# Weight blocks side by side instead of in pairs, moving tiles 96 bytes higher, and v normalised in eight pieces

## The chip, the core and the metric

The kernel runs on one core of a Trainium2 chip. The metric is the device time of one execution in microseconds: 2833.92 us is the median of three runs of the kernel before (2832.6 to 2835.17).

Five engines work side by side: TensorE (matmuls, PE in the profile; its weight loads are listed apart as PEld), VectorE (DVE), ScalarE (ACT), GpSimd (POOL) and SyncE (SP), which issues most of the DMAs. Data lies in a memory of 128 partitions (SBUF); matmuls write to another one (PSUM).

## What is computed

One step of a two-layer streaming encoder in float32, on 256 frames of a new stream and 32 frames of a running one, 288 columns in all, of width 2048. Layer 0 mixes frames with a gated MLP (gMLP), layer 1 with a multi-scale retention; each is followed by a SwiGLU network of hidden width 5632, and each of the four sublayers by a residual and a LayerNorm.

```python
def gmlp_mix(x, w_in, ln_g, ln_b, w_s, b_s, w_out):
    z = jax.nn.gelu(x @ w_in, approximate=False)
    u, v = jnp.split(z, 2, axis=-1)
    v = layer_norm(v, ln_g, ln_b)
    ...
    mixed = jnp.einsum('gts,bnsgc->bntgc', w, vg) + bias
    s = u * mixed.reshape(bsz, t, GMLP_HALF)
    return s @ w_out, v

def swiglu(x, w_in, w_out):
    gate, up = jnp.split(x @ w_in, 2, axis=-1)
    return (jax.nn.silu(gate) * up) @ w_out

def trunk(...):
    for i in range(DEPTH):
        if i % N_MIXERS == 0:
            h, v = gmlp_mix(...)
        else:
            h, s = retention_mix(...)
        x = layer_norm(ALPHA * x + h, ln_mix_g[i], ln_mix_b[i])
        x = layer_norm(ALPHA * x + swiglu(x, w_ffn_in[i], w_ffn_out[i]), ln_ffn_g[i], ln_ffn_b[i])
```

## The kernel before

**Weights.** All matrices are cut into blocks of 128 x 128, and the host packs them, in the order in which the kernel uses them, into chunks of eight (`CB`). `Core.prep` loads a chunk of 512 KB with a DMA on SP's queue into a tile `raw` (three buffers), and `split` makes two tiles of it in a shorter float32 format that TensorE takes in one pass (`F32R`): `whi` is the rounded chunk, made by ScalarE, and `wlo` what is left of it, made by VectorE. Both have four buffers, and a chunk is prepared three chunks ahead of its use.

**Matmuls.** `step` multiplies one weight block with one 128-row slice of the activations, which exist as a pair of tiles as well (`xh`, `xl`): three matmuls, hi by hi (L106), hi by lo (L107) and lo by hi (L108), summed into the same PSUM bank. Each has a block of weights of its own to load, so there is a load for every matmul. `Core.tiles` and `Core.group` run the steps over all slices of an output tile of 128 rows. After each output tile a clock of the program, `tick`, runs what was put off with `after(n, ...)`, n output tiles ahead.

**Where the bytes lie.** A block of weights is not contiguous in its chunk: blocks 2i and 2i+1 share 256 columns, the one taking the even columns and the other the odd ones (L89); the host packs them so. The activations that stream through TensorE, called moving tiles, have rows of 320 floats (`ROW`) of which the first four are left free (`LEAD`). A step of 288 columns reads such a row turned: `turned` (L168) takes four floats, leaves out eight, and so on, three times over the row, and writes the results to PSUM in the same order. Steps of 290 columns carry two columns more, for the gain and bias of a LayerNorm that is corrected after the matmul; they read the row straight. These are the first twelve output tiles after each of three LayerNorms. Tiles that nobody reads, such as `shift` with 64 floats, move all tiles that are allocated behind them: `xh`, `xl`, `y`, and the tiles of the gMLP, the retention and the ffn. The pool of the weights is allocated earlier.

**The gMLP's v.** The 16 output tiles of v come first, then those of u, all within layer 0's first matrix. v is transposed to rows through DRAM, its statistics are taken, and `v_norm` normalises it in quarters of 512 columns, for 32 and twice 128 rows: a scaling on ScalarE, a product with the gain and a sum with the bias on VectorE, and for the 32 rows of the running stream a split. Gain and bias come by a DMA on SP's queue into `gb`, two buffers. The first quarter is normalised at once, the others two, four and six output tiles later; four output tiles behind each quarter, `sample_mix` uses the running stream's part.

**What sets the order.** TensorE runs its instructions in the order of the code. On the other engines a scheduler puts the instructions in order when the program is built.

Of the kernel before, what the change touches and what calls it, by code (L numbers as in the profile page):

```python
# [10 lines left out]
F32 = mybir.dt.float32  # L11
# [8 lines left out]
P = 128  # L20
# [18 lines left out]
CB = 8  # L39
# [7 lines left out]
class Core:  # L47
# [33 lines left out]
    def blk(self, w, k, m):  # L81
        i = len(self.order)
        self.order.append((w, k, m))
        c, j = divmod(i, CB)
        if j == 0:
            self.prep(c + 3)
            self.ready.pop(c - 1, None)
        hi, lo = self.ready[c]
        return tuple(t[:, j // 2 * 2 * P + j % 2:(j // 2 + 1) * 2 * P:2] for t in (hi, lo))  # L89

    def state(self, h):

# [80 lines left out]
def rsqrt(nc, out, v, t):  # L173

    nc.vector.tensor_scalar(out.bitcast(I32), v.bitcast(I32), -0.5, float(0x5F3759DF), ALU.mult, ALU.add)
    for _ in range(3):
        newton(nc, out, out, v, t)
# [242 lines left out]
def moving(pool, n, name, tag=None):  # L420

    t = pool.tile([P, n, ROW], F32R, name=name, **({"tag": tag} if tag else {}))
    return t[:, :, LEAD:]


def split(nc, hi, lo, f):
    nc.scalar.copy(hi, f)  # L427
    nc.vector.tensor_tensor(lo, f, hi.bitcast(F32), ALU.subtract)  # L428
# [12 lines left out]
def gmlp(core, cst, x, y, lnp, ins, v_out, load):  # L441
# [3 lines left out]
    with ExitStack() as es:  # L445
        pool = es.enter_context(tc.tile_pool(name="gm", bufs=1, reuse_waits="tile"))
# [46 lines left out]
        def v_rows(q):  # L493
            for t in range(3):
                n = rows[t]
                nc.vector.bn_stats(st[:n, t, q, :], vt[t][:n, q * 512:(q + 1) * 512])
            if q == 3:
                v_stats()

        def v_stats():  # L500
            for t in range(3):
                n = rows[t]
                nc.vector.bn_aggr(nrm[:n, t, 0:2], st[:n, t, :, :].rearrange("p a b -> p (a b)"))
            mean, var, u, r, w, b = (nrm[:, :, i] for i in (0, 1, 2, 3, 4, 5))
            nc.vector.tensor_scalar(u, var, LN_EPS, None, ALU.add)
            rsqrt(nc, r, u, w)
            nc.vector.scalar_tensor_tensor(b, mean, -1.0, r, ALU.mult, ALU.mult)
            v_norm(0)
            for q in range(1, 4):
                core.after(2 * q, lambda q=q: v_norm(q))  # L510

        def v_norm(q):
            cs = slice(q * 512, (q + 1) * 512)
            gb = pool.tile([P, 2, 512], F32, tag="gb", name=f"gb{q}", bufs=2)
            nc.sync.dma_start(gb, ins["a_gb"][:, :, cs])
            for t in (2, 0, 1):
                n = rows[t]
                v = vt[t][:n, cs]
                nc.scalar.activation(v, v, AF.Identity, bias=nrm[:n, t, 5:6], scale=nrm[:n, t, 3:4])
                nc.vector.tensor_tensor(v, v, gb[:n, 0, :], ALU.mult)  # L520
                nc.vector.tensor_tensor(v, v, gb[:n, 1, :], ALU.add)
                if t == 2:
                    split(nc, v3[:NS, cs], v3[NS:2 * NS, cs], v)
                    nc.scalar.copy(v3[2 * NS:, cs], v)
            core.after(4, lambda: sample_mix(q))
            if q == 3:
                nc.gpsimd.dma_start(v_out, vs[:NS, :])

        def sample_mix(q):

            ps = core.bank(f"smix{q}")
            for g in (2 * q, 2 * q + 1):
                w = w3[:, g].rearrange("p a n -> p (a n)")
                nc.tensor.matmul(ps[:, (g % 2) * 256:(g % 2 + 1) * 256], w, v3[:, g * 256:(g + 1) * 256], start=True, stop=True)
            view = ps.rearrange("p (m a s) -> p m a s", a=4, s=32)
            for a in range(4):
                r = slice(32 * a, 32 * a + 32)
                nc.vector.transpose(ms[r, 4 * q:4 * q + 4, :], view[r, :, a, :])
# [30 lines left out]
def ffn(core, cst, x, y, lnp, layer, prev, out=None):  # L569
    tc, nc = core.tc, core.nc  # L570
    xh, xl = x
    xs = lambda k: (xh[:, k, :NT], xl[:, k, :NT])
    ln = PostNorm(core, cst, x, y, lnp, 2 * layer + 1, out)
    with tc.tile_pool(name=f"ffn{layer}", bufs=1, reuse_waits="tile") as pool:
        hh = moving(pool, HH, f"hh{layer}")
        hl = moving(pool, HH, f"hl{layer}")
        for half in range(2):
            sg = {}

            def evac(m, ps):  # L580
                if m < HT:
                    t = pool.tile([P, NT], F32, tag="sg", name=f"sg{layer}_{m}", bufs=4)
                    nc.scalar.activation(t, ps[:, :NT], AF.Silu)
                    sg[m] = t
                else:
                    j = m - HT
                    i = j - half * HH
                    f = pool.tile([P, NT], F32, tag="hf", name=f"hf{layer}_{j}", bufs=3)
                    nc.vector.tensor_tensor(f, ps[:, :NT], sg.pop(j), ALU.mult)
                    split(nc, hh[:, i, :NT], hl[:, i, :NT], f)  # L590

            ms = []
            for j in range(half * HH, (half + 1) * HH):
                ms += [j, HT + j]
            if half == 0:
                prev.start(f"f_in{layer}", ms, evac)
                ms = ms[4 * RAW:]
            core.tiles(f"f_in{layer}", 0, list(range(KT)), ms, xs, evac, grouped=False)
            core.tiles(f"f_out{layer}", half * HH, list(range(HH)), list(range(KT)),
                       lambda k: (hh[:, k, :NT], hl[:, k, :NT]),  # L600
                       ln.last if half else ln.part)
    return ln
# [297 lines left out]
@with_exitstack  # L900
def hybrid_step(ctx, tc, ins, outs):
    nc = tc.nc
    ctx.enter_context(tc.manual_schedule(engines={PE}))
    core = Core(ctx, tc, ins["wpack"])
    cp = ctx.enter_context(tc.tile_pool(name="cp", bufs=1))
    lnp = ctx.enter_context(tc.tile_pool(name="lnp", bufs=1))
    cp.tile([P, 64], F32, name="shift")
    lnp.tile([P, 32], F32, name="shift_lnp")
    xh = moving(cp, KT, "xh")
    xl = moving(cp, KT, "xl")  # L910
    y = cp.tile([P, KT, NT], F32, name="y")
    cst = {}
    cp.tile([P, 32], F32, name="shift_one")
    cst["one2048"] = cp.tile([P, P], F32, name="one2048")
    nc.gpsimd.memset(cst["one2048"], 1.0 / D)
    cst["ln"] = cp.tile([P, 4, 2, KT], F32, name="lnv")
    cst["one_r"] = cp.tile([P, P], F32R, name="one_r")
    nc.scalar.copy(cst["one_r"], cst["one2048"])
    warm = core.bank("warm")
    for _ in range(11):  # L920
        nc.tensor.matmul(warm[:, :P], cst["one2048"], cst["one2048"], start=True, stop=True)

    def load(k):
        if k < KT:
            if k % 2 == 0:
                nc.sync.dma_start(y[:, k:k + 2, :], ins["xT"][:, k:k + 2, :])
            split(nc, xh[:, k, :NT], xl[:, k, :NT], y[:, k, :])

    with tc.manual_schedule(engines={mybir.EngineType.DVE, mybir.EngineType.Activation}):
        core.prep(0, lambda: load(0))  # L930
        for k in range(1, 4):
            load(k)
            core.prep(k)
    x = (xh, xl)
    ln = gmlp(core, cst, x, y, lnp, ins, outs["v"], lambda s: load(s + 4))
    ln = ffn(core, cst, x, y, lnp, 0, ln)
    ln = retention(core, cst, x, y, lnp, ln, ins, outs["st_p"], outs["st_s"])
    ffn(core, cst, x, y, lnp, 1, ln, outs["yT"])
    core.flush()
    assert len(core.order) == NBLK + NSTATE  # L940
    return core.order
# [85 lines left out]
```

## Time and profile before

| what | value |
|---|---|
| median of three runs | 2833.92 us (2832.6 to 2835.17) |
| profiled execution, first to last instruction | 2831.8 us |
| what lies around it, by the median | 2.1 us |
| TensorE busy | 2818.8 us, 21,574 matmuls |
| VectorE busy | 1696.5 us |
| ScalarE busy | 1241.5 us |
| moved by DMA | 515.49 MB, 182 GB/s on average |

The time of the profiled execution itself isn't given beside its span; the median less the span stands in for what lies around it. In a row of the groups, the number behind `x` counts the instructions, and behind the bar stand the time in which at least one of them ran, the mean duration of one in ns, and the idle time ahead of them. Names are those of the program: `af_in` is an output of a step in an ffn's first matrix, `aa_in` of the gMLP's, `ab_in` of the retention's. A matmul of float32 proper counts twice, since TensorE runs it in two passes. In a row of stretches, the number behind an engine's busy time counts the instructions that touch the stretch.

### The profile page before, as it was taken

To read this page: it belongs to the slowest core of one execution; us is meant where nothing else is said; L and a number is where in the kernel's file an instruction comes from. 1 tells how busy PE (TensorE), PEld (TensorE's weight loads), DVE (VectorE), ACT (ScalarE), POOL (GpSimd) and SP (SyncE) were. 2 spreads that over 40 slices of the span, in tenths; PEclk is the share of its full clock that TensorE was granted. 3 is DMA by queue.
4 is the path that set the end of the run, shared out by engine and by line. 5 is a ranking of instruction groups with operands and counts; after the bars stand their busy time and mean duration, and the time that the engine had idled before them with its cause. 6 is when DMAs were issued, how large, how long until landed. Compare 5 with 4: busy or idle time off the path is not lost.

```text
span 2831.8 us, 51419 instructions
## 1 busy us (share of the span) xinstructions
PE 2818.8 (100%) x21574; PEld 2804.0 (99%) x21574; DVE 1696.5 (60%) x2432; ACT 1241.5 (44%) x1642; POOL 141.4 (5%) x241
## 2 busy tenths in 40 slices
PE   9999999999999999999999999999999999999998
PEld 9999999999999999999999999999999999999998
DVE  5678864444444456777765666767854444444455
ACT  5544553333333344554443444444553333333343
POOL 1100000000000000012200111200000000000001
PEclk9999999999999999999999999999999999999999
DMA  8655555555555555567765666755555555555553
GB/s 281 208 177 164 166 167 172 171 171 170 170 168 171 174 174 173 174 207 230 226 195 169 195 214 214 223 190 170 164 171 170 170 170 171 171 172 172 171 170 125
DMA packets 146584, 515.49 MB, mean 182 GB/s; under 512 B 18016, under 2 KB 20336, under 8 KB 146320
## 3 DMA queue, kind: packets, MB, share of 16 engines
q1 hardware_dynamic: 131984, 473.47, 50.9%
q0 software_dynamic: 14224, 38.59, 4.5%
q8 instruction: 168, 2.75, 0.4%
q14 instruction: 64, 0.52, 0.1%
q10 hardware_dynamic: 144, 0.15, 0.0%
HBM read 486.98 MB, written 25.17 MB: 181 GB/s over the span
## 4 chain that ended last, share of the span: by engine, by line
PE 98%; DVE 1%; DMA 1%; ACT 0%; issue 0%; POOL 0%; SPq 0%; DVEq 0%; POOLq 0%; ACTq 0%
PE af_in L108 13%; PE af_in L107 13%; PE af_in L106 13%; PE ab_in L106 7%; PE ab_in L108 7%; PE ab_in L107 7%; PE af_out L107 6%; PE af_out L108 6%; PE af_out L106 6%; PE ab_out L108 2%; PE ab_out L106 2%; PE ab_out L107 2%; PE aa_in L108 2%; PE aa_in L107 2%; PE aa_in L106 2%; PE aa_out L108 1%
## 5 line engine op out<-in xcount | busy, mean ns | idle before, releaser
L428 DVE TENSOR_TENSOR wlo<-raw,whi 128x1024 fp32r<-128x1024 f32 (+1 forms) x892 | 1085.5, 1219 | 903.2 <-ACT whi L427 898.9
L427 ACT CAST whi<-raw 128x1024 fp32r<-128x1024 f32 (+1 forms) x892 | 933.0, 1048 | 1434.0 <-PE af_in L107 343.0
L107 PE MATMUL af_in<-xl,whi 128*128 128x288 f32 (+1 forms) x2816 | 825.1, 293 | 0.0
L108 PE MATMUL af_in<-xh,wlo 128*128 128x288 f32 (+1 forms) x2816 | 823.3, 292 | 0.0
L106 PE MATMUL af_in<-xh,whi 128*128 128x288 f32 (+1 forms) x2816 | 820.8, 291 | 0.0
L108 PEld LDWEIGHTS af_in<-xh,wlo 128*128 128x128 f32 x2816 | 550.5, 196 | 0.0
L107 PEld LDWEIGHTS af_in<-xl,whi 128*128 128x128 f32 x2816 | 545.8, 194 | 0.0
L106 PEld LDWEIGHTS af_in<-xh,whi 128*128 128x128 f32 x2816 | 544.1, 193 | 0.0
L108 PE MATMUL ab_in<-xh,wlo 128*128 128x288 f32 (+1 forms) x1536 | 449.6, 293 | 0.0
L106 PE MATMUL ab_in<-xh,whi 128*128 128x288 f32 (+1 forms) x1536 | 449.3, 293 | 0.0
L107 PE MATMUL ab_in<-xl,whi 128*128 128x288 f32 (+1 forms) x1536 | 447.7, 291 | 0.0
L107 PE MATMUL af_out<-hl,whi 128*128 128x288 f32 x1408 | 411.0, 292 | 0.0
L108 PE MATMUL af_out<-hh,wlo 128*128 128x288 f32 x1408 | 409.9, 291 | 0.0
L106 PE MATMUL af_out<-hh,whi 128*128 128x288 f32 x1408 | 409.8, 291 | 0.0
L106 PEld LDWEIGHTS ab_in<-xh,whi 128*128 128x128 f32 x1536 | 299.7, 195 | 1.1
L108 PEld LDWEIGHTS ab_in<-xh,wlo 128*128 128x128 f32 x1536 | 297.8, 194 | 0.0
L107 PEld LDWEIGHTS ab_in<-xl,whi 128*128 128x128 f32 x1536 | 296.8, 193 | 0.9
L108 PEld LDWEIGHTS af_out<-hh,wlo 128*128 128x128 f32 x1408 | 273.9, 195 | 0.0
L107 PEld LDWEIGHTS af_out<-hl,whi 128*128 128x128 f32 x1408 | 273.4, 194 | 0.0
L106 PEld LDWEIGHTS af_out<-hh,whi 128*128 128x128 f32 x1408 | 271.8, 193 | 0.0
L108 PE MATMUL aa_in<-xh,wlo 128*128 128x288 f32 x512 | 149.4, 292 | 1.1 <-DVE wlo L428 1.1
L107 PE MATMUL aa_in<-xl,whi 128*128 128x288 f32 x512 | 149.5, 292 | 0.1
(249 smaller groups left out, 2942.6 us busy)
## 6 DMA issues: line engine op xcount, KB each, us to landing
raw<-in_wpack_dram SPq DMA_DIRECT2D x887, 512.0 KB, 3.4
v_room<-tv POOLq DMA_DIRECT2D x32, 144.0 KB, 4.7
of<-o_room POOLq DMA_DIRECT2D x32, 144.0 KB, 4.4
vw<-v_room POOLq DMA_DIRECT2D x8, 512.0 KB, 5.6
out_st_s_dram<-sso POOLq DMA_DIRECT2D x16, 256.0 KB, 2.7
o_room<-to POOLq DMA_DIRECT2D x8, 512.0 KB, 3.9
out_st_p_dram<-so POOLq DMA_DIRECT2D x16, 256.0 KB, 5.5
y<-in_xT_dram SPq DMA_DIRECT2D x8, 288.0 KB, 5.0
```

What stands on the lines that cost most here:

```text
L106: mm(ps, hi, xh, start=first, stop=False)
L107: mm(ps, hi, xl, start=False, stop=False)
L108: mm(ps, lo, xh, start=False, stop=last)
L427: nc.scalar.copy(hi, f)
L428: nc.vector.tensor_tensor(lo, f, hi.bitcast(F32), ALU.subtract)
```

## The change

Three things are changed. The blocks of a chunk lie side by side, 128 contiguous columns each, in the kernel and in the host's packing (the blocks of the retention's state lay so before, and still do). `shift` has 88 floats instead of 64, which moves all tiles behind it by 96 bytes. And v is normalised in eight pieces of 256 columns, one after each of the next eight output tiles, with four buffers of half the size for gain and bias; `sample_mix` follows two output tiles after each second piece, and so at the same output tiles as before.

```diff
@@ blk
-        return tuple(t[:, j // 2 * 2 * P + j % 2:(j // 2 + 1) * 2 * P:2] for t in (hi, lo))
+        return tuple(t[:, j * P:(j + 1) * P] for t in (hi, lo))
@@ v_stats
-            v_norm(0)
-            for q in range(1, 4):
-                core.after(2 * q, lambda q=q: v_norm(q))
+            for i in range(8):
+                core.after(1 + i, lambda i=i: v_norm(i))
 
-        def v_norm(q):
-            cs = slice(q * 512, (q + 1) * 512)
-            gb = pool.tile([P, 2, 512], F32, tag="gb", name=f"gb{q}", bufs=2)
+        def v_norm(i):
+            cs = slice(i * 256, (i + 1) * 256)
+            gb = pool.tile([P, 2, 256], F32, tag="gb", name=f"gb{i}", bufs=4)
             nc.sync.dma_start(gb, ins["a_gb"][:, :, cs])
...
-            core.after(4, lambda: sample_mix(q))
-            if q == 3:
+            if i % 2:
+                core.after(2, lambda: sample_mix(i // 2))
+            if i == 7:
                 nc.gpsimd.dma_start(v_out, vs[:NS, :])
@@ hybrid_step
-    cp.tile([P, 64], F32, name="shift")
+    cp.tile([P, 88], F32, name="shift")
@@ kernel
-            pairs = wpack[c].reshape(P, CB // 2, P, 2)
-            pairs[:, j // 2, :, j % 2] = mats[w][k * P:(k + 1) * P, m * P:(m + 1) * P]
+            wpack[c, :, j * P:(j + 1) * P] = mats[w][k * P:(k + 1) * P, m * P:(m + 1) * P]
```

The order on TensorE and GpSimd is the same before and after. On VectorE, this stands before where v is normalised; `raw`, `whi` and `wlo` ending in 1524 to 1526 are chunk 42, `gb_1339` and `gb_1479` the first two quarters' gain and bias:

```order
L521 TENSOR_TENSOR y<-y,gb_1479 32x512
L520 TENSOR_TENSOR g_vp<-g_vp,gb_1479 128x512 x2
L428 TENSOR_TENSOR g_v_149<-y,g_v_149 32x512
L521 TENSOR_TENSOR g_vp<-g_vp,gb_1479 128x512 x2
L428 TENSOR_TENSOR wlo_1526<-raw_1524,whi_1525 128x1024
L428 TENSOR_TENSOR wlo_1559<-raw_1557,whi_1558 128x1024
L428 TENSOR_TENSOR wlo_1589<-raw_1587,whi_1588 128x1024
L538 STREAM_TRANSPOSE g_ms<-smix_1619 32x128 x4
```

Three chunks' splits follow each other behind two quarters. After, at the same place (`gb_1479` and `gb_1556` are now the second and third of eight, 1571 to 1573 is chunk 43):

```order
L520 TENSOR_TENSOR y<-y,gb_1479 32x256
L519 TENSOR_TENSOR g_vp<-g_vp,gb_1479 128x256 x2
L520 TENSOR_TENSOR g_vp<-g_vp,gb_1479 128x256 x2
L428 TENSOR_TENSOR g_v_149<-y,g_v_149 32x256
L428 TENSOR_TENSOR wlo_1526<-raw_1524,whi_1525 128x1024
L519 TENSOR_TENSOR y<-y,gb_1556 32x256
L519 TENSOR_TENSOR g_vp<-g_vp,gb_1556 128x256
L520 TENSOR_TENSOR y<-y,gb_1556 32x256
L520 TENSOR_TENSOR g_vp<-g_vp,gb_1556 128x256
L519 TENSOR_TENSOR g_vp<-g_vp,gb_1556 128x256
L428 TENSOR_TENSOR g_v_149<-y,g_v_149 32x256
L520 TENSOR_TENSOR g_vp<-g_vp,gb_1556 128x256
```

The split of chunk 42 still stands behind two pieces, which are half as wide; then comes the third piece, ahead of the split of chunk 43.

On SP's queue, before, the last two quarters' gain and bias stand together behind the loads of chunks 43 and 44:

```order
L73 DMA raw_1557<-in_wpack_dram 128x1024
L73 DMA raw_1587<-in_wpack_dram 128x1024
L515 DMA gb_1626<-in_a_gb_dram 128x2x512
L515 DMA gb_1776<-in_a_gb_dram 128x2x512
L73 DMA raw_1641<-in_wpack_dram 128x1024
L73 DMA raw_1671<-in_wpack_dram 128x1024
```

After, the last four of the eight are spread over five loads of chunks:

```order
L73 DMA raw_1601<-in_wpack_dram 128x1024
L514 DMA gb_1717<-in_a_gb_dram 128x2x256
L514 DMA gb_1804<-in_a_gb_dram 128x2x256
L73 DMA raw_1655<-in_wpack_dram 128x1024
L514 DMA gb_1888<-in_a_gb_dram 128x2x256
L73 DMA raw_1685<-in_wpack_dram 128x1024
L73 DMA raw_1732<-in_wpack_dram 128x1024
L514 DMA gb_1974<-in_a_gb_dram 128x2x256
L73 DMA raw_1762<-in_wpack_dram 128x1024
```

Each of these waits until a piece of v has freed its buffer; the loads of chunks 45, 46 and 48 now stand behind such a wait, where before the load of chunk 45 alone stood behind both.

## The prediction

> **What bounds the kernel now.** I read the page's first part and its chain of waits, then the groups of instructions by form, then stretches of single stages, and last the few places where a matmul of the main stream stands next to another kind.
>
> ```profile
> span 2831.8 us, 51419 instructions
> PE 2818.8 (100%) x21574; PEld 2804.0 (99%) x21574; DVE 1696.5 (60%) x2432; ACT 1241.5 (44%) x1642; POOL 141.4 (5%) x241
> PEclk9999999999999999999999999999999999999999
> PE 98%; DVE 1%; DMA 1%; ACT 0%; issue 0%; POOL 0%; SPq 0%; DVEq 0%; POOLq 0%; ACTq 0%
> ```
>
> TensorE is the path: 98% of the chain, at its full granted clock. So the time is the number of matmuls times their spacing, plus a head, a tail and a few waits. A matmul's recorded duration holds its pipeline too, so the spacing is taken from stretches of one stage.
>
> ```profile
> L107 PE MATMUL af_in<-xl,whi 128*128 128x288 f32 x2432 | 710.6, 292 | 0.0
> L108 PE MATMUL af_in<-xh,wlo 128*128 128x288 f32 x2432 | 708.8, 291 | 0.0
> L106 PE MATMUL af_in<-xh,whi 128*128 128x288 f32 x2432 | 706.4, 290 | 0.0
> ...
> L108 PE MATMUL ab_in<-xh,wlo 128*128 128x288 f32 x1344 | 392.6, 292 | 0.0
> ...
> L108 PE MATMUL af_in<-xh,wlo 128*128 128x290 f32 x384 | 114.5, 298 | 0.0
> ...
> L108 PE MATMUL ab_in<-xh,wlo 128*128 128x290 f32 x192 | 57.0, 297 | 0.0
> ...
> L294 PE MATMUL m<-s,one_r 128*128 128x288 f32 x16 | 2.8, 294 | 0.0
> ...
> L267 PE MATMUL cen<-cen,one_r 128*128 128x288 f32 x4 | 1.2, 295 | 0.0
> ```
>
> ```profile
> core 0: us, PE busy (x) PEld busy (x) DVE busy (x) ACT busy (x) POOL busy (x), PEclk, DMA share, GB/s
> 315.00:385.00 70.00, 70.00 (x522) 70.00 (x521) 56.68 (x97) 43.45 (x68) 0.58 (x1) 1.00 0.49 161
> 600.00:720.00 120.00, 120.00 (x933) 120.00 (x932) 59.91 (x70) 41.08 (x39) 0.00 (x0) 1.00 0.51 169
> ...
> 126.00:158.00 32.00, 30.88 (x239) 30.44 (x238) 30.36 (x49) 24.70 (x35) 0.51 (x1) 1.00 0.53 181
> ```
>
> The three lines of `step` (L106 to L108) run 7,040 times each, 21,120 matmuls in all (the code's NBLK: 512 + 256 + 1,536 + 512 + 4,224 blocks). Two forms occur. The 288-column form reads its moving tile turned (16 bytes, then a jump of 48); the 290-column form, at the start of the two ffn layers and of the retention, reads it straight, 3 x (384 + 192) = 1,728 times by the two groups above. That leaves 19,392 turned ones. From 600 to 720 us some 931 turned matmuls start (933 touch the stretch, two of them across its edges): 120 us / 931 = 128.9 ns each. From 315 to 385 us it is 70 us / 520 = 134.6 ns for a straight one. The difference, 5.7 ns, is about that of the durations, 298 against a mean of 291.3 over the groups of the turned form. So a duration in ns can serve as a yardstick for spacing where only a few rows exist: one ns longer is one ns later, and one ns on all step matmuls is 21.1 us, 0.75% of the time. The stretch of 600 to 720 us has VectorE busy half the time, that of 315 to 385 us four fifths, and both come out as steady as the group means; what the other engines do is not what sets the spacing.
>
> **The change part by part.** No matmul is added or removed, and TensorE's order stays as it is. What changes is which bytes each one reads.
>
> *Weight blocks side by side.* While a matmul streams, the weights of the next are loaded. Now these 128 columns lie 8 bytes apart over 1,024 bytes; then they lie 4 bytes apart over 512. No step matmul of this trace does that, so its price has to come from the neighbours. Other matmuls of the kernel have weights stored contiguously (the score, value and state products of the retention, the LayerNorm sums), and the last step matmul ahead of such a block is exactly the case wanted: turned moving data, and a contiguous load of 128 columns beneath it. These are three of the sixteen ahead of the output and state products, and one ahead of a load of 64 columns:
>
> ```profile
> L108 PE MATMUL ab_in<-xh,wlo 128*128 128x288 f32 x1 | 0.3, 294 | 0.0
> ...
> L820 PE MATMUL ob<-vv,ph 128*128 128x512 f32 x1 | 0.4, 388 | 0.0
> L108 PE MATMUL ab_in<-xh,wlo 128*128 128x288 f32 x1 | 0.3, 295 | 0.0
> ...
> L870 PE MATMUL sp<-vv,kh 128*128 128x512 f32 x1 | 0.4, 388 | 0.0
> L108 PE MATMUL ab_in<-xh,wlo 128*128 128x288 f32 x1 | 0.3, 295 | 0.0
> ...
> L107 PE MATMUL ab_in<-xl,whi 128*128 128x288 f32 x1 | 0.3, 291 | 0.0
> L108 PE MATMUL ab_in<-xh,wlo 128*128 128x288 f32 x1 | 0.3, 290 | 0.0
> ```
>
> They took 294, 295 and 295 ns (in the groups of single moments at 1251.3, 1859.5 and 1867.8 us), where the group of the same line has 292 and all turned ones 291.3; above the 64-column load (the last pair of rows, at 1243.6 us) it took 290. So the load is felt by the matmul above it, and a contiguous one more than a paired one. These rows give +2 to +3.7 ns.
>
> The straight form says the opposite. The LayerNorm sums have straight moving data of 288 columns and contiguous weights, and took 294 to 295 ns; the straight step matmuls have pairs, and took 297 to 298 with two columns more, which at 128.9 / 288 = 0.45 ns a column is 296.8 for 288. Side by side is cheaper there by some 2.3 ns. The loads themselves speak that way too:
>
> ```profile
> L106 PEld LDWEIGHTS af_in<-xh,whi 128*128 128x128 f32 x2816 | 544.1, 193 | 0.0
> L870 PEld LDWEIGHTS sp<-vv,kh 128*128 128x128 f32 x64 | 11.6, 188 | 2.1
> L820 PEld LDWEIGHTS ob<-vv,ph 128*128 128x128 f32 x48 | 8.6, 188 | 1.4
> ```
>
> A contiguous load takes 188 ns, a paired one 193 and more. But a load is begun a matmul ahead, and what counts is the matmul. So the price lies between -2.3 and +3.7 ns. I take +2.6 for the turned form (294.2 less the mean of 291.3 and the 292 of the same line), because those rows share the moving pattern with 19,392 of the 21,120, and -2.3 for the 1,728 straight ones: 19,392 x 2.6 ns = +50.4 us and 1,728 x -2.3 ns = -4.0 us.
>
> Here a rule of the Trainium skill speaks for no change at all: its page "TensorE: Matmul & The Clock Gate" (section "Step-by-step: what each phase is for") says that TensorE reads moving data and weights through two independent ports, so that loading the next weights takes nothing from the running matmul. By it this part costs 0 instead of the +46 us above. The rows of 290 and 294 to 295 ns do not agree with it.
>
> *Moving tiles 96 bytes higher.* `shift` grows from 256 to 352 bytes, and with it every later tile, among them all that the step matmuls stream and none of the weights, whose pool comes first. In the trace of before all streamed tiles of the step stand alike against the weights, since rows and tiles are multiples of 128 bytes long, so no row shows another distance. Its bounds are those of the whole pattern: nothing, down to the 2.3 ns that the straight rows would allow, or up to the loss of what turning wins, 296.8 - 291.3 = 5.5 ns. I take 0, nearest to the rows that I priced the load from, and keep 5.5 as the upper end.
>
> *v normalised in eight pieces.* The page's step of four pieces sits at 126 to 158 us, where the stretch above has TensorE busy for 30.88 of 32 us, and VectorE for 30.36.
>
> ```profile
> PE aa_in L108 <- DVE wlo L428: 1.1, 2, 1.0
> L428 DVE TENSOR_TENSOR wlo<-raw,whi 128x256 fp32r<-128x256 f32 x4 | 1.5, 420 | 3.8 <-ACT whi L427 3.8
> L521 DVE TENSOR_TENSOR g_vp<-g_vp,gb 128x512 f32<-128x512 f32 x8 | 5.4, 684 | 0.1
> 134.83 1.30 DVE L521 TENSOR_TENSOR g_vp<-g_vp,gb 128x512 f32<-128x512 f32 x2
> 136.04 2.35 DVE L428 TENSOR_TENSOR wlo<-raw,whi 128x1024 fp32r<-128x1024 f32 x2
> ```
>
> TensorE waits 1.1 us here for `wlo`, which VectorE makes only after two pieces of v in a row. Eight pieces make 56 instructions on VectorE instead of 28: 56 x 420 - 28 x 684 ns = +4.4 us in a stretch where VectorE has 1.6 us to spare, and about as many more on ScalarE, which has 7 us. Cover: the weights are prepared three chunks ahead, each 24 x 128.9 ns = 3.1 us long, and in the order of after the split of chunk 42 still stands behind two pieces, now of half the width. On SP's queue the loads of g and b become eight of half the size, and the later four each wait for a buffer that a piece of v has read, with the raw weights queued behind them; before, two did. If the wait only moves, nothing changes; if all the extra work is uncovered, +4.4 us; if the wait goes, -1.1. I take -1.
>
> **The sum.** +50.4 - 4.0 + 0 - 1 = +45.4 us. On the profiled execution's span of 2831.8 us that is 2877.2; the median of the three runs, 2833.92, stands 2.1 us above that span, so 2879 us, slower by 1.6%.
>
> **The rivals.**
>
> *The shorter load wins (faster).* If what the straight rows and the load rows show holds for the turned form as well, every step matmul gets 2.3 ns shorter: 21,120 x 2.3 = 48.6 us, so 2833.9 - 48.6 - 1 = 2784 us. For it: 188 against 193 ns, and 294.5 against 296.8. Against it: the rows of 294 and 295 ns above turned data. It decides from the point where the mean duration of the turned form falls below 291.0 (0.27 ns x 21,120 = 5.7 us).
>
> *Nothing happens (same).* The load is hidden whatever its layout, and only v moves: 2833 us. For it: the spacing of 128.9 ns is steady over the stages, so one could take it for a property of the streaming alone. Against it: the 290 of the 64-column load. This is what the rule of the two ports in the Trainium skill would give, and the page "SBUF — State Buffer" (section "Specifications (TRN2)", the row on cachelines) has both layouts read each line of 16 bytes at least twice, and so at full rate.
>
> *Turning loses its effect (much slower).* Turned data is 5.5 ns faster than straight under paired weights. That may rest on both streams stepping through the memory in a fixed relation, which the change breaks twice, by the other step of the weights and by the 96 bytes. Then a turned matmul costs what a straight one does: 19,392 x 5.5 = 106.7 us, 2833.9 + 106.7 - 4 - 1 = 2936 us. For it: the only known contrast of patterns in the trace is that large. Against it: the 294 and 295 ns, which keep half of the gain.
>
> **How the numbers follow.** My forecast has 0.66, the faster rival 0.14, no change 0.05, the loss of turning 0.12, and 0.03 is left for more than that. Within the forecast, between +1 and +4 ns a matmul, the time lies from 2850 to 2915 us. The range of 2830 to 2945 leaves out the faster rival and the last 0.03. A difference under 0.2% (5.7 us) can't be told from no change with this kernel. Slower is forecast, loss of turning and the rest, 0.81; same 0.05; faster 0.14.
>
> **What the profile after would show.** If the first part is right, the groups of L106 to L108 with 128x288 read 293 to 295 ns instead of 290 to 292, evenly over all stages; a stretch such as 600 to 720 us has some 914 matmuls instead of 933; the straight groups of 290 columns read about 295; the loads of L106 to L108 drop from 193 to about 188 ns; the wait of aa_in for `wlo` at 136 us is gone or half as long. The granted clock stays full, VectorE and ScalarE have the same work and lower shares. Durations below 291 mean the faster rival, of 296 or more the lost turning. If the three lines differ by more than now, the 96 bytes act on the streamed tile, and not the layout of the weights. What would make this wrong: the rows that I lean on are transitions between two kinds of matmul, not a steady stream, and a steady stream may settle into another rhythm.

## The result

The kernel after takes 2787.49 us (median of four runs, 2787.04 to 2790.12) against 2834.26 us of the kernel before: a ratio of 0.9834 with a 95% interval of 0.982 to 0.9848, so 1.7% faster. The forecast was 2879 us, slower. The time is within 4 us of the rival called "the shorter load wins" (2784 us), though the runs below show that its mechanism is not the one at work.

The profile after: the page's first part, its clock row and its chain of waits.

```profile
span 2787.7 us, 51475 instructions
PE 2775.6 (100%) x21574; PEld 2760.2 (99%) x21574; DVE 1698.1 (61%) x2460; ACT 1245.7 (45%) x1662; POOL 141.8 (5%) x241
PEclk9999999999999999999999999999999999999999
PE 98%; DVE 1%; DMA 0%; issue 0%; POOL 0%; ACT 0%; DVEq 0%; POOLq 0%
```

TensorE is the path as before, with as many matmuls, at its full granted clock, with 43 us less busy time. So the matmuls follow each other more closely. The groups by form of the kernel after, with one group of weight loads at the end:

```profile
L106 PE MATMUL af_in<-xh,whi 128*128 128x288 f32 x2432 | 701.1, 288 | 0.0
L107 PE MATMUL af_in<-xl,whi 128*128 128x288 f32 x2432 | 701.1, 288 | 0.0
L108 PE MATMUL af_in<-xh,wlo 128*128 128x288 f32 x2432 | 701.1, 288 | 0.0
...
L108 PE MATMUL af_in<-xh,wlo 128*128 128x290 f32 x384 | 113.5, 296 | 0.0
...
L294 PE MATMUL m<-s,one_r 128*128 128x288 f32 x16 | 2.8, 297 | 0.0
L267 PE MATMUL cen<-cen,one_r 128*128 128x288 f32 x4 | 1.2, 294 | 0.0
...
L106 PEld LDWEIGHTS af_in<-xh,whi 128*128 128x128 f32 x2816 | 528.5, 188 | 0.0
```

The turned form reads 288 ns on all three lines, where 290 to 292 stood before, the straight one 296 for 298, the loads 188 for 193. The stretches of the kernel after that answer to those of before:

```profile
126.00:158.00 32.00, 32.00 (x253) 31.78 (x252) 31.38 (x73) 29.30 (x54) 0.00 (x0) 1.00 0.52 174
315.00:385.00 70.00, 70.00 (x527) 70.00 (x526) 58.62 (x102) 44.84 (x73) 0.00 (x0) 1.00 0.47 164
600.00:720.00 120.00, 120.00 (x950) 120.00 (x949) 61.53 (x72) 42.30 (x41) 0.00 (x0) 1.00 0.50 174
...
1135.00:1205.00 70.00, 69.60 (x521) 68.84 (x521) 54.99 (x100) 44.36 (x73) 3.78 (x6) 1.00 0.53 176
```

As in the prediction, two of the matmuls that touch a stretch only reach over its edge. From 600 to 720 us, 120 us / 948 = 126.6 ns, for 128.9 before; the starts taken from the trace give 126.67 against 128.89, and both are even over the whole stretch: every three matmuls take 380.0 ns after, and 386.7 before (456 and 464 of the cycles in which some expectations below count). The difference, 2.22 ns x 19,392 turned matmuls, is 43.1 us. From 315 to 385 us the straight form needs 70 / 525 = 133.3 ns for 134.6, 1.3 ns x 1,152 in the two ffn layers = 1.5 us. In the stretch of v TensorE has no idle time left (32.00 of 32 us, 30.88 before), and a new pause stands where the retention begins, 0.4 us of the last row. A matmul's record is some 160 ns longer than the spacing, so idle time shows a short pause only in part. By the starts, the pauses at v cost 1.7 us before and 0.2 after, a gain of 1.5 us, and the new ones at the retention cost 1.3 us. Together 43.1 + 1.5 + 1.5 - 1.3 = 44.8 us; the spans differ by 44.1 and the medians by 46.8.

Of the signs that the prediction named, the loads of 188 ns and the wait for `wlo` came as written, the durations below 291 point to the faster rival, and one sign was of no use: the three lines differ less than before, and still the 96 bytes act, as the runs show.

### The profile page after: what moved, and what is told of

The parts are those of the page before. It is cut to its first block, busy times and chain, and to the rows that moved or that the text cites. A ratio compares the mean times of both kernels' runs of the same rounds, so it can differ in the third digit from the quotient of the medians.

```text
span 2787.7 us, 51475 instructions
## 1 busy us (share of the span) xinstructions
PE 2775.6 (100%) x21574; PEld 2760.2 (99%) x21574; DVE 1698.1 (61%) x2460; ACT 1245.7 (45%) x1662; POOL 141.8 (5%) x241
## 4 chain that ended last, share of the span: by engine, by line
PE 98%; DVE 1%; DMA 0%; issue 0%; POOL 0%; ACT 0%; DVEq 0%; POOLq 0%
PE af_in L108 13%; PE af_in L107 13%; PE af_in L106 13%; PE ab_in L106 7%; PE ab_in L107 7%; PE ab_in L108 7%; PE af_out L108 6%; PE af_out L107 6%; PE af_out L106 6%; PE aa_in L108 2%; PE aa_in L107 2%; PE ab_out L107 2%; PE aa_in L106 2%; PE ab_out L108 2%; PE ab_out L106 2%; PE aa_out L108 1%
## 5 line engine op out<-in xcount | busy, mean ns | idle before, releaser
L107 PE MATMUL af_in<-xl,whi 128*128 128x288 f32 (+1 forms) x2816 | 814.8, 289 | 0.0
L108 PE MATMUL af_in<-xh,wlo 128*128 128x288 f32 (+1 forms) x2816 | 814.6, 289 | 0.0
L108 PEld LDWEIGHTS af_in<-xh,wlo 128*128 128x128 f32 x2816 | 528.5, 188 | 0.0
L107 PEld LDWEIGHTS af_in<-xl,whi 128*128 128x128 f32 x2816 | 528.5, 188 | 0.0
L106 PEld LDWEIGHTS af_in<-xh,whi 128*128 128x128 f32 x2816 | 528.5, 188 | 0.0
L107 PEld LDWEIGHTS ab_in<-xl,whi 128*128 128x128 f32 x1536 | 288.3, 188 | 2.2 <-DVE xl L428 1.1
L106 PEld LDWEIGHTS ab_in<-xh,whi 128*128 128x128 f32 x1536 | 288.3, 188 | 1.1
L108 PEld LDWEIGHTS ab_in<-xh,wlo 128*128 128x128 f32 x1536 | 288.2, 188 | 0.0
L107 PEld LDWEIGHTS af_out<-hl,whi 128*128 128x128 f32 x1408 | 263.8, 187 | 0.0
L108 PEld LDWEIGHTS af_out<-hh,wlo 128*128 128x128 f32 x1408 | 263.8, 187 | 0.0
L106 PE MATMUL aa_in<-xh,whi 128*128 128x288 f32 x512 | 148.6, 290 | 0.0
```

The lines of the kernel that those rows point to most:

```text
L106: mm(ps, hi, xh, start=first, stop=False)
L107: mm(ps, hi, xl, start=False, stop=False)
L108: mm(ps, lo, xh, start=False, stop=last)
```

## The experiments

Theory A is the faster rival: a contiguous block is loaded sooner, and that shortens every matmul above it. Theory B: what counts is where the streamed bytes lie relative to the bytes of the load beneath them, so the layout and the 96 bytes act only together. Each run has a run of the kernel before beside it on the same chip (medians 2836.2 to 2837.8 us in these jobs), and ratios are against that.

### The three parts, one at a time

Layout alone, on the kernel before (the host's packing is changed with it):

```diff
-        return tuple(t[:, j // 2 * 2 * P + j % 2:(j // 2 + 1) * 2 * P:2] for t in (hi, lo))
+        return tuple(t[:, j * P:(j + 1) * P] for t in (hi, lo))
```

> Side-by-side weights alone (shift stays at 64 floats, v in four pieces). Theory A, the shorter load: a contiguous block shortens every matmul above which it is loaded, wherever the tiles lie. Then this edit gives all of the gain but the wait at 136 us: 19,392 turned matmuls x (128.9 - 126.7 = 2.2 ns) = 43 us and some 2 us of the straight ones, 2834.3 - 45 = about 2789 us, turned groups at 288 ns. Theory B, the distance: what counts is how the streamed bytes lie against the weights' bytes, and the layout gains only together with the 96 bytes. Then this kernel is at 2834 us or above; the rows of 294 to 295 ns that the prediction leaned on had contiguous weights at just this distance, so up to 2834 + 50 = 2885 us, and turned groups of 291 to 295 ns.

The 96 bytes alone:

```diff
-    cp.tile([P, 64], F32, name="shift")
+    cp.tile([P, 88], F32, name="shift")
```

> The 96 bytes alone (weights in pairs, v in four pieces). Theory A: no change, 2834 us, turned groups at 291 ns, 128.9 ns apart. Theory B: a new distance gives pairs another rhythm too; one step of 8 cycles of 1.2 GHz in three matmuls is 6.7 ns, 47 us over 7,040 steps, so 2787 or 2881 us, or more steps than one.

v in eight pieces alone: the diff of `v_stats` and `v_norm`, without the other two.

> v in eight pieces alone (pairs, shift 64 floats). All theories: between 0 and -1.6 us, 2833 us, not to be told from no change by the time. In the trace the wait of aa_in for wlo near 136 us (1.1 us) is gone. My prediction's bounds were -1.1 and +4.4 us.

| kernel | median us | ratio to before, 95% interval |
|---|---|---|
| layout alone | 2819.47 | 0.994 (0.9926 to 0.9954) |
| 96 bytes alone | 2887.46 | 1.0181 (1.0167 to 1.0195) |
| v in eight pieces alone | 2832.60 | 0.9988 (0.998 to 0.9997) |
| all three (after) | 2787.49 | 0.9834 (0.982 to 0.9848) |

If the parts added up, they would give -0.6 + 1.8 - 0.1 = +1.1%; together they give -1.7%. The 96 bytes cost 51 us with pairs and bring about 30 us with blocks side by side (from 0.994 x 0.9988 to 0.9834 is -0.95%, or -27 us; the medians of the two kernels differ by 32, of which v is 1 to 4). So theory A, which asked for 2789 us of the layout alone, fails, and the sign of the second part depends on the first. With layout alone, the groups by form differ from stage to stage:

```profile
L108 PE MATMUL af_in<-xh,wlo 128*128 128x288 f32 x2432 | 702.8, 289 | 0.0
L108 PE MATMUL af_out<-hh,wlo 128*128 128x288 f32 x1408 | 408.4, 290 | 0.0
L106 PE MATMUL ab_in<-xh,whi 128*128 128x288 f32 x1344 | 394.0, 293 | 0.0
L107 PE MATMUL ab_in<-xl,whi 128*128 128x288 f32 x1344 | 393.3, 293 | 0.0
L108 PE MATMUL ab_in<-xh,wlo 128*128 128x288 f32 x1344 | 393.0, 292 | 0.0
...
L106 PEld LDWEIGHTS af_in<-xh,whi 128*128 128x128 f32 x2816 | 529.8, 188 | 0.0
```

A stretch of the retention's output matrix in the same kernel:

```profile
1470.00:1550.00 80.00, 80.00 (x617) 80.00 (x616) 44.11 (x54) 26.72 (x26) 0.00 (x0) 1.00 0.52 168
```

The ffn's first matrix gains, the retention loses (292 and 291 ns before; 80 / 615 = 130.1 ns of spacing), and the loads take 188 ns in both. The time of a load is not what sets the spacing.

Of v, the waits and the stretch of the kernel with that part alone show that the pause is gone, at a span of 2830.6 us for 2831.8:

```profile
PE warm L921 <- POOL g_nrm L476: 1.0, 1, 1.0
```

```profile
126.00:158.00 32.00, 32.00 (x251) 32.00 (x251) 30.82 (x77) 28.20 (x53) 0.00 (x0) 1.00 0.58 182
```

The wait of `aa_in` for `wlo` is no longer listed, and the 1.12 us of idle time are used. It isn't gone for good: in the run of after with four matmuls more (below), which has the same program up to there, `aa_in` waits 0.3 us for `wlo` again. The longer interval of the time (0.03 to 0.2%) holds this value and doesn't narrow it.

### Why one kernel has two speeds: a rhythm that holds

With layout alone, the second half of the first ffn's output matrix changes its speed in the middle, on the same tiles. TensorE's instructions in order of time, with start and duration in us:

```profile
1029.62 0.29 PE L106 MATMUL af_out<-hh,whi 128*128 128x288 f32 x1
1029.75 0.29 PE L107 MATMUL af_out<-hl,whi 128*128 128x288 f32 x1
1029.87 0.29 PE L108 MATMUL af_out<-hh,wlo 128*128 128x288 f32 x1
1030.00 0.29 PE L106 MATMUL af_out<-hh,whi 128*128 128x288 f32 x1
...
1030.38 0.29 PE L267 MATMUL cen<-cen,one_r 128*128 128x288 f32 x1
1030.52 0.29 PE L106 MATMUL af_out<-hh,whi 128*128 128x288 f32 x1
1030.65 0.29 PE L107 MATMUL af_out<-hl,whi 128*128 128x288 f32 x1
1030.78 0.29 PE L108 MATMUL af_out<-hh,wlo 128*128 128x288 f32 x1
1030.91 0.29 PE L106 MATMUL af_out<-hh,whi 128*128 128x288 f32 x1
```

Ahead of the matmul `cen`, which belongs to a LayerNorm, three step matmuls take 0.38 us (126.7 ns each); behind it they take 0.39 (130.0 ns each), and so on for the remaining 726 matmuls of the stage. The same happens at the same place of the second ffn. Hence theory R: at this distance several rhythms are stable (a rhythm is a spacing that the stream of steps keeps up), and a foreign matmul, one that belongs to no step, throws the stream from one into another. Against it stands theory T, that the traffic of other engines changes there. The test puts four such matmuls elsewhere into the kernel with layout alone:

```diff
         mm(ps, lo, xh, start=False, stop=last)
+        if w[:4] == "f_in" and self.seen(w) in (256, 880):
+            mm(self.bank(f"probe{len(self.order)}")[:, :NT], self.one_r, x[0][:, :NT], start=True, stop=True)
```

> The layout alone again (shift 64), with one more matmul in each half of each ffn's first matrix, four in all: 288 columns of xh, read straight, against one_r, into a bank that nobody reads. It stands where the stream ran at 126.7 ns without it. Theory R, rhythm: the step stream has more than one stable rhythm at this distance, 126.7 and 130.0 ns, and one foreign matmul throws it from one into the other, as the one at 1030.4 us (cen) did. Then the rest of each half and of the following half of the second matrix runs at 130.0 ns: (448 + 352 + 528 + 109) steps x 3 x 2 layers x 3.3 ns = 28 us, 2819 + 28 = about 2847 us; from 750 to 900 us near 1154 matmuls touch the stretch in place of 1185. Theory T, traffic: what changed at 1030.4 us was the work of the other engines at the end of the layer. Then four matmuls cost 0.5 us, about 2820 us, and the groups of the ffn keep 289 and 290 ns.

The same edit, on the kernel after:

> The kernel after with the same four additional matmuls that cost the layout alone some 28 us at shift 64. If the distance of after has 126.7 ns as the one rhythm to which the stream returns: 2787.5 + 4 x 0.14 = about 2788 us, and the stretch of 750 to 900 us still has 1186 matmuls. If 126.7 is only the one that it happened to fall into: up to 2815 us.

Layout alone with the four matmuls took 2847.62 us (1.0039, 1.0025 to 1.0054), so four matmuls cost 28 us, as R had it. After with the four took 2789.56 us (0.9838, 0.9821 to 0.9854). The same three stretches, all within an ffn's first matrix, for layout alone, for layout alone with the four, and for after with the four; the first lies behind the first additional matmul, the second ahead of the second one (in after that one falls into its end), the third behind it:

```profile
480.00:580.00 100.00, 100.00 (x792) 100.00 (x791) 47.06 (x51) 39.78 (x49) 0.00 (x0) 1.00 0.55 174
735.00:790.00 55.00, 55.00 (x437) 55.00 (x436) 25.98 (x28) 21.78 (x27) 0.00 (x0) 1.00 0.53 174
800.00:975.00 175.00, 175.00 (x1384) 175.00 (x1383) 81.84 (x86) 70.16 (x87) 0.00 (x0) 1.00 0.53 174
```

```profile
480.00:580.00 100.00, 100.00 (x771) 100.00 (x770) 46.00 (x49) 38.73 (x48) 0.00 (x0) 1.00 0.50 169
735.00:790.00 55.00, 55.00 (x426) 55.00 (x425) 25.37 (x26) 20.78 (x27) 0.00 (x0) 1.00 0.50 169
800.00:975.00 175.00, 175.00 (x1360) 175.00 (x1360) 81.23 (x85) 68.67 (x85) 0.00 (x0) 1.00 0.51 172
```

```profile
480.00:580.00 100.00, 100.00 (x791) 100.00 (x791) 47.21 (x51) 40.20 (x50) 0.00 (x0) 1.00 0.52 173
735.00:790.00 55.00, 55.00 (x436) 55.00 (x435) 26.32 (x29) 21.84 (x27) 0.00 (x0) 1.00 0.52 173
800.00:975.00 175.00, 175.00 (x1384) 175.00 (x1383) 81.64 (x87) 70.28 (x87) 1.10 (x2) 1.00 0.53 175
```

Layout alone runs at 126.6 ns in all three (100 / 790). With the additional matmuls the first stretch is at 130.0 (100 / 769), the second still is, and only the next foreign matmul moves the stream again, to 128.9 (175 / 1358). So R's rule holds, but two parts differ from what was written: the slow rhythm was carried over into the next half, and the second matmul threw the stream into a third rhythm. The two about cancel, and that the sum of 28 us came out is in part luck. At the distance of after the same matmuls leave nothing behind in the turned stream. VectorE, ScalarE and the DMAs are no busier with the four matmuls than without in these stretches (a DMA share of 0.50 for 0.55 in the first), and the 2820 us that T asked for are missed by 28: T is out.

### Distance or place

Both streams 96 bytes higher, with the layout alone: a tile that nobody reads is put ahead of the weights' pool.

```diff
+        pad = ctx.enter_context(tc.tile_pool(name="pad", bufs=1))
+        pad.tile([P, 24], F32, name="pad")
         self.wp = ctx.enter_context(tc.tile_pool(name="wp", bufs=4))
```

> The layout alone (shift 64, v in four pieces), with a tile of 96 bytes that nobody reads ahead of the weights' pool: weights and moving tiles both lie 96 bytes higher. Theory D, distance between the two streams: nothing changes against the layout alone, about 2819 us with its mixture of 126.7, 128.9 and 130.0 ns. Theory P, place: what counts is where the moving tiles lie in the memory, and they lie now where after has them: about 2789 us, all turned groups at 288 ns.

2820.92 us (0.9946, 0.9926 to 0.9966), as with the layout alone. The moving tiles lie here at the addresses that they have in after, so their place alone does nothing; their distance from the weights does.

Other distances for the kernel after: `shift` at 72, 80, 96, 104, 112 and 120 floats, and once eight free floats ahead of each row (`LEAD = 8`), which moves the rows by 16 bytes more than after does. And one more for pairs, on the kernel before.

> The kernel after with shift at 72 floats: the moving tiles 32 bytes above those of before, where after has them 96 above. Theory A (only the load counts) is out by the layout's run alone. Theory B, distance: each distance has its own set of rhythms, in steps of 8 cycles of 1.2 GHz in three matmuls (456, 464, 468 and 480 were seen). I expect a mixture, 2787 to 2835 us.

> Shift at 80 floats, 64 bytes above. Theory B: if the 126.7 ns of after need exactly its distance, this is 2800 to 2835 us; if a wide band of distances gives them, 2787 us.

> Shift at 96 floats, 128 bytes above. As for 80 floats: 2787 us if the band reaches here, up to 2835 us if not. A time below 2780 us would say that 126.7 ns is no floor.

> The kernel after with shift at 104 floats, 160 bytes above before's tiles. Distances at 0, 32, 64, 96, 128 and 192 bytes gave turned matmuls at 126.7/128.9/130.0, 130.0, 130.7, 126.7, 130.0 and 130.0 ns. If the 126.7 ns come back every 128 bytes, this one answers to 32 bytes: 2852 us. If the memory repeats only within 256 bytes, no bound but those rhythms: 2787 to 2865 us.

> The kernel after with shift at 112 floats, 192 bytes above before's (after has 96). By the runs at 64, 72, 80, 88 and 96 floats (2819, 2852, 2864, 2787, 2853 us) most distances sit near 130.0 ns: about 2852 us. If the pattern repeats within 128 bytes, as 72 and 96 might hint, it answers to 80 floats: 2864 us.

> Shift at 120 floats, 224 bytes above before's tiles and 128 above after's. If the pattern repeats within 128 bytes: 2787 us, turned groups at 288 ns, as after. If not: 2850 to 2865 us, as most distances.

> The kernel after with eight free floats ahead of each row instead of four: all streamed rows start 16 bytes further, 112 above before's in place of 96. If the band of 126.7 ns is 32 bytes wide or more: 2787 us. If it is as narrow as 16 bytes: 2850 us or more, towards the 130.0 ns of 128 bytes. Below 2780 us the floor would be lower than 126.7 ns.

> The kernel before (pairs) with shift at 72 floats, 32 bytes up. Is the layout needed for 126.7 ns, or do pairs only lack the right distance? Pairs took 128.9 ns at 0 and 131.4 at 96 bytes. If the layout is needed, 128.9 ns or more here too: 2834 us or above. If any layout has its distances: possibly 2787 us.

Bytes are counted from where the moving rows stand before. The third column is the number of matmuls that touch the stretch of 600 to 700 us, all of them turned, the fourth 100 us divided by that number less two. One matmul more or less is 0.17 ns in it: by the starts, the rows of 129.9 and 130.0 are all 130.0 ns, 64 bytes take 130.7 and 224 bytes 129.7.

| kernel | median us | matmuls | ns each |
|---|---|---|---|
| side by side, 0 (layout alone) | 2819.47 | 792 | 126.6, elsewhere to 130 |
| side by side, 32 bytes | 2852.13 | 772 | 129.9 |
| side by side, 64 | 2864.17 | 768 | 130.5 |
| side by side, 96 (after) | 2787.49 | 792 | 126.6 |
| side by side, 112 (`LEAD = 8`) | 2859.65 | 771 | 130.0 |
| side by side, 128 | 2852.66 | 771 | 130.0 |
| side by side, 160 | 2854.38 | 771 | 130.0 |
| side by side, 192 | 2865.13 | 771 | 130.0 |
| side by side, 224 | 2844.73 | 774 | 129.5 |
| pairs, 0 (before) | 2834.26 | 778 | 128.9 |
| pairs, 32 | 2877.93 | 765 | 131.1 |
| pairs, 96 | 2887.46 | 763 | 131.4 |

Of nine distances with blocks side by side, two are faster than before and seven slower. The good one is narrow, 16 bytes further it is lost, and it does not come back 128 bytes further (224 bytes: 129.7 ns by the starts). The loads take 187 to 189 ns at all nine. Pairs had 126.7 ns at none of three distances; whether they have it at another was not tried. The total also hides which form pays. 192 bytes took what the guess of a repetition gave (2865 for 2864 us), but by luck: against 64 bytes, with 192 the turned form is faster and the straight one slower. The straight stretch with 64 and with 192 bytes:

```profile
315.00:385.00 70.00, 70.00 (x527) 70.00 (x526) 57.53 (x96) 43.69 (x68) 0.58 (x1) 1.00 0.50 166
```

```profile
315.00:385.00 70.00, 70.00 (x502) 70.00 (x501) 56.29 (x94) 41.56 (x65) 0.58 (x1) 1.00 0.47 157
```

That is 133.3 and 140.0 ns.

### The order in which a row is read

All on the kernel after. Each edit changes the order in which a matmul's results are written to PSUM along with the order of reading, since `step` turns both alike. Straight instead of turned (`if False:` in place of the test for 288 columns), and three other ways of turning:

```diff
-    return v.rearrange("p (g a c) -> p a g c", a=3, c=4)
+    return v.rearrange("p (g a c) -> p a g c", a=9, c=4)
```

with `a=9, c=4`, then `a=3, c=8`, then `a=6, c=4`.

> The kernel after, with all step matmuls reading their rows straight instead of turned (same sums, other order of columns). Theory A: straight matmuls over a contiguous load run as the 1,728 of the kernel after do, 133.3 ns apart for 290 columns, 132.4 for 288: 19,392 x (132.4 - 126.7 = 5.7 ns) = 111 us, so about 2898 us. Theory B with a fixed relation of the two streams as its cause: turning mattered only under pairs, and straight is now as fast, 2790 us.

> The kernel after with rows read in another order: four floats, then a jump over 32 (9 x 16 bytes from one group to the next), nine times over the row, in place of three. If only the distance of the first bytes counts: 2787 us. If the whole pattern of the streamed addresses against the loaded ones counts: another rhythm, by the straight form's 133.3 ns as the worst seen, up to 19,392 x 6.6 = 128 us more, and no bound on the side of a gain but the 120 ns that 288 columns take at the full clock.

> The kernel after with rows read eight floats at a time (32 bytes, then a jump of 64) in place of four, three times over the row as before. Strides of 16 bytes (straight) and of 144 bytes gave 133.3 ns, of 48 bytes 126.7. If collisions between the two streams set the rhythm, this order may be better or worse than 48 bytes: between the 120 ns that 288 columns take at the full clock (2787 - 129 = 2658 us) and the straight form's 2921 us; if single places of 16 bytes in steps of 48 are what avoids them, it is near the straight form's.

> The kernel after with a jump twice as long: four floats, then 96 bytes to the next group, six times over the row. The same bounds, 2658 to 2921 us. If an odd number of 16-byte places is what makes 48 bytes good, 96 bytes is worse than 126.7 ns, and the time is above 2850 us.

| order | median us | ratio, 95% interval | ns each, 600 to 700 us |
|---|---|---|---|
| 16 bytes every 48 (after) | 2787.49 | 0.9834 (0.982 to 0.9848) | 126.6 |
| 32 bytes every 96 | 2828.62 | 0.9973 (0.9961 to 0.9986) | 128.9 |
| 16 bytes every 144 | 2914.18 | 1.0275 (1.0255 to 1.0296) | 133.3 |
| straight | 2920.78 | 1.0308 (1.0289 to 1.0326) | 133.3 |
| 16 bytes every 96 | 3559.05 | 1.2551 (1.2515 to 1.2587) | 166.7 |

Straight rows lie above both numbers expected (2898 and 2790 us). Most of the 23 us above the first is that 288 columns take as long as 290 did, 133.3 ns and not 132.4 (0.9 ns x 19,392 = 18 us); and the gMLP's first matrix took 135.1 ns a matmul, by the starts in the trace. Turning is worth more after the change than before (133.3 - 126.6 = 6.7 ns, for 5.7, where the straight rows had two columns more): it isn't a remedy for pairs alone. No order beat the one of after. The last row is the strongest sign of how much the order matters; the stretch and a group of it:

```profile
600.00:700.00 100.00, 100.00 (x602) 100.00 (x601) 36.10 (x39) 30.43 (x38) 0.00 (x0) 1.00 0.40 132
```

```profile
L106 PE MATMUL af_in<-xh,whi 128*128 128x288 f32 x2432 | 821.9, 338 | 0.0
...
L106 PE MATMUL af_in<-xh,whi 128*128 128x290 f32 x384 | 113.3, 295 | 0.0
```

Only the turned form is slow; the straight one takes 131.1 ns by the starts, even less than in after (133.3). All these orders read each 16 bytes in four steps in a row. The Trainium skill's page "SBUF — State Buffer" (section "Specifications (TRN2)") has reading at full rate wherever a line of 16 bytes is hit at least twice; by it the reading would cost all five the same. They lie up to 40 ns apart, so that rule is not enough to price an order. Whether the reading or the writing to PSUM makes the difference no run here shows, since both were changed at once.

## Why the prediction was wrong

**What bounds the kernel: right.** TensorE's spacing sets the time before and after, and the granted clock is full. The statement that other engines don't set the spacing holds too.

**Duration as a yardstick for spacing: right in sign, too large.** The turned form's duration fell from 291.3 to about 288.3 ns, by 3, its spacing by 2.22. Across kernels it can mislead: with `LEAD = 8` the first line of `af_in` reads 291 ns, about as before, at 130.0 ns of spacing instead of 128.9.

**Side by side, +2.6 ns on the turned form: the step that failed.** It was taken from rows of 294 and 295 ns, the last step matmuls ahead of a contiguous load. The layout alone, at the distance at which these rows stood, shows what they were worth: in the retention, where they come from, the layout is slower indeed, by 1.1 ns (130.0 for 128.9), in the ffn it is faster by 2.2, and the whole kernel is 17 us faster, where the two terms of the layout in the sum had made it 46 us slower. The rows belong to the edge of the stream and not to the layout: in the kernel after, where every block is contiguous, the eight step matmuls ahead of an `ob` matmul still last 294 ns on average, while the stream that they end lasts 288 to 289. What the steady stream costs depends on the rhythm into which it falls, which these rows can't show. The caveat at the end of the prediction named this, and the sum did not use it. This term and that of the 96 bytes, +50.4 and 0 in the sum, together measured -2.22 ns x 19,392 = -43.1 us on the turned form.

**Straight matmuls, -2.3 ns: right in sign.** Their duration fell by 2 ns, their spacing in the ffn by 1.3, and in the retention not at all (133.4 and 133.3 ns by the starts).

**The 96 bytes, priced at 0: wrong.** They cost 51 us with pairs and bring about 30 with blocks side by side. Per turned matmul that is +2.5 ns in the one case, and -3.3 ns in the other wherever the slow rhythm ruled, so the bounds given (-2.3 and +5.5 ns) were passed below. The argument that no row shows another distance was true; a price of 0 does not follow from it, and a chance for both signs, in each layout, was missing. Nothing in the trace of before could have told the sign. But it did show that form, layout and distance don't fix a spacing: its straight matmuls take 134.7 ns in the two ffn layers and 133.4 in the retention, by the starts.

**v in eight pieces, -1 us: right.** The idle time of 1.1 us is gone, in the run with that part alone and in after, with VectorE at 31.38 us of 32 in that stretch, so the additional work found its place, if only just: the run of after with the four matmuls has 0.3 us of the wait left.

**The rivals.** "The shorter load wins" came within 4 us of the time by luck, with the wrong cause: 188 ns stand beside every spacing from 126.6 to 133.3 ns. "Nothing happens" rested on the rule of the two independent ports (Trainium skill, "TensorE: Matmul & The Clock Gate", section "Step-by-step: what each phase is for"). The runs do not agree with it: moving one stream against the other by 16 bytes changes the spacing from 126.6 to 130.0 ns, moving both together changes nothing. "Turning loses its effect" was right that the two streams stand in a relation which the change alters, and wrong in its sign.

**What stays open.** The runs show that the spacing depends on distance, layout, order and history. Where in the chip the two streams meet, why 96 bytes is the good distance, what part the order of writing to PSUM has, and whether an order below 126.6 ns exists, they don't tell. A model of it fit to these numbers would be argued, not shown.

## What to carry to other kernels

Where matmuls and weight loads run back to back, the addresses are a tuning parameter of their own: sweep the distance between streamed rows and weights in steps of 16 or 32 bytes, anew after every change of layout or reading order, since the sign of one depends on the other. Judge a spacing from stretches of every stage, and after a foreign matmul too: a fast rhythm that one matmul can break is worth less than one to which the stream returns. And don't price a steady stream by the rows at its edges.

## What the hardware showed that was not expected

- The stream of matmuls has a memory. With the layout alone, with and without the four matmuls, three rhythms occur in the ffn at the same distance, 126.7, 128.9 and 130.0 ns, and each lasted for hundreds of matmuls until a foreign one came.
- These are 380.0, 386.7 and 390.0 ns for three matmuls, and the straight form of after takes 400.0, all whole multiples of 3.33 ns; one such step is 1.1 ns a matmul, 23 us on 21,120. It isn't a rule for every stream: pairs with the 96 bytes average 394.3 ns, and the straight matmuls of before 404.0 in the ffn.
- The straight form has two rhythms at the distance of after as well. It takes 133.3 ns in after and 131.1 in the runs with 32 bytes every 96 and 16 bytes every 96; the run of after with the four matmuls has 131.1 in the first ffn layer, ahead of the first of the four (534 matmuls in the 70 us in which after has 525), and 133.3 in the second.
- Four matmuls of 0.13 us each made a kernel 28 us slower; at another distance the same four cost nothing that stands out of the noise (ratios to before of 0.9838 and 0.9834, spans of 2786.6 and 2787.7 us).
- A step of 96 bytes instead of 48 between groups of 16, in reading and in writing, put the turned matmuls 40 ns further apart and made the kernel after 772 us longer.
